# A list scheduler's view of row groups, 64-row transfers, f32 products and VectorE beside GpSimd, in a streaming encoder layer

## The chip, the cores and the metric

The kernel runs on one core of a Trainium2 chip. The metric is the device time of one execution in microseconds (us). The engines are TensorE (PE: matmuls and transposes; PEld: its weight loads), VectorE (DVE), ScalarE (ACT), GpSimd (POOL) and SyncE (SP), which here only issues DMA transfers. ScalarE issues some transfers as well. Each engine takes its own instructions strictly in the order in which the program lists them; semaphores hold an instruction back until what it needs is there.

## The reference

One layer of a streaming encoder over 2048 prompt rows and 64 sample rows of 1024 columns, all in float32:

```python
def encoder_layer(x, c, conv_hist, attend, p):
    mod = jax.nn.silu(c) @ p['w_ada'] + p['b_ada']
    sh1, sc1, gt1, sh2, sc2, gt2 = [m[:, None, :] for m in jnp.split(mod, 6, axis=-1)]
    h = rms_norm(x, p['norm1_g']) * (1 + sc1) + sh1
    z = h @ p['w_in']
    glu_a, glu_b, q, k, v, g_conv, g_attn = jnp.split(z, offs, axis=-1)
    u = glu_a * jax.nn.sigmoid(glu_b)
    conv_out, conv_state = conv_module(u, conv_hist, ...)   # depthwise conv of 31 taps, LayerNorm, swish, projection
    q = rms_norm(q.reshape(B, T, N_HEADS, HEAD_DIM), p['q_norm_g'])
    k = rms_norm(k.reshape(B, T, N_HEADS, HEAD_DIM), p['k_norm_g'])
    o = attend(q, k, v, p['rel_bias']).reshape(B, T, ATTN_DIM)   # own chunk of 64 rows and 8 before it
    merged = jax.nn.sigmoid(g_conv) * conv_out + jax.nn.sigmoid(g_attn) * (o @ p['w_attn_out'])
    x = x + gt1 * (merged @ p['w_o'])
    h2 = rms_norm(x, p['norm2_g']) * (1 + sc2) + sh2
    gate, up = jnp.split(h2 @ p['w_ffn_in'], 2, axis=-1)
    x = x + gt2 * ((jax.nn.silu(gate) * up) @ p['w_ffn_out'])
    return x, conv_state, k, v
```

`mod`, the modulation, is a product of the condition vectors c with `w_ada`. Its first two parts, `sh1` and `sc1`, are in every row of `h`, and so in everything that comes after it.

## The kernel before

**Stages.** The first stage goes through the rows in four blocks (576, 512, 512 and 512): `h` from x, the input projection, the convolution, the attention by heads, the gates. The results go to DRAM scratch. The second stage goes through them in three blocks (576, 768, 768): merge, output projection, norm, FFN. Big products are made three times with operands that are split into a high and a low part (`split`: ScalarE copies the high part, VectorE or GpSimd subtracts it), so that each weight passes through ScalarE and VectorE or GpSimd before TensorE can use it.

**The start.** `load_vectors` (line 1101) loads two small tiles: `r0` (16 rows: 8 of c_prompt, 8 of c_sample, on ScalarE's queue) and `r1` (76 rows, on SyncE's queue: norm1_g in rows 0 to 8, norm2_g to 16, b_dw to 20, conv_ln_g to 24, conv_ln_b to 28, b_ada to 76). In the trace both are called `r`. `Slabs` loads pieces of `w_ada` (`wmod`, 512 KB each, four held) on both queues in turn, `first_rows` (1227) the first 576 rows of x, on both queues, and `Weights` pieces of `w_in` (`wst`, three held). `first_block` (1232) then works in this order. TensorE transposes `r0`; ScalarE and VectorE make silu(c) of it (`cl`); TensorE multiplies `wmod` by `cl` (`mod_sums`, tile `pa`); it transposes `r1` (`vectors`), which gives `cols`; it turns the sums into columns with the 0/1 matrix `sel` (`mod_columns`), and VectorE adds `b_ada` and the gains: tiles `A` and `B`. Beside it ScalarE sums the squares of the rows of x (`junk`, `ssq`), GpSimd takes the power, VectorE scales the rows (`scale_rows`). TensorE transposes them (`turn`), VectorE applies `A` and `B` (`h`), ScalarE and VectorE split it into `hh` and `hl`, and the first product of the projection reads `hh` and `whi`.

**The planner.** The order on each engine is not that of the code. `Meter` and `Queue` hand each operation to `Plan.do` (line 239), which records it with an estimated cost; `flush` (300) puts all the operations of a stage into an order, engine by engine, with a simulation of its own, and then emits them in that order (all lines of the trace are therefore line 383). There are three flushes: line 1962, near the end of the first stage, line 1990 at its end, and line 2561 at the end of the kernel.

- `places` (177) names the regions that an operand touches. For a tile in SBUF they are groups of 32 partitions by 32 columns. Two operations that touch one region, one of them writing, get an edge. A transfer's edge is always a true wait (`deps`): it is planned only after the end of the other.
- `cost` (201) gives the time that an operation holds its engine (`occ`) and the time until its result is there (`lat`).
- `do` gives a transfer its `size`, the time that it is to take of one shared server, by its bytes and by the length of its contiguous runs.
- In `flush` each operation gets a due time, from TensorE's clock (the sum of TensorE's costs in the order of the code) backwards through all who read its result; a transfer's due time is 8 us earlier still. TensorE's operations are ranked by the order of the code, those of the other engines by due time. Then the operation that can start first is placed again and again, at equal start the one of lower rank.
- `room` (392) holds a transfer back while eight others of its queue are planned to be in flight, and an operation whose tile has no free buffer.
- `place` (407) sets start and end, and takes a transfer's size from the server.

The planner's estimates change nothing but the order. Which waits the program contains is decided by the tile framework, which tracks overlaps by itself.

Of the kernel before, what the change touches and what calls it, by code (L numbers as in the profile page):

```python
# [17 lines left out]
P = 128  # L18
# [67 lines left out]
class Meter:  # L86


    def __init__(self, engine, name, stream, plan):
        self.engine, self.name, self.stream, self.plan = engine, name, stream, plan  # L90
# [35 lines left out]

class Op:

    __slots__ = ("engine", "call", "occ", "lat", "deps", "at", "tiles", "start", "end", "need", "ready", "out", "order", "rank", "size", "clock")

    @property
    def ins(self):
# [3 lines left out]
class Rooms:  # L136
# [6 lines left out]
    def tile(self, shape, dtype, tag=None, name=None, bufs=None):  # L143
        kw = {k: v for k, v in (("tag", tag), ("name", name), ("bufs", bufs)) if v is not None}
        t = self.pool.tile(shape, dtype, **kw)
        self.plan.opened(t, (self.key, tag or name), bufs or self.bufs, self.psum)
        return t


# [9 lines left out]
class Plan:  # L159
# [3 lines left out]

    def __init__(self, tc):
        self.tc, self.on, self.ops, self.behind = tc, False, [], []
        self.clock, self.pools, self.flight = 0.0, 0, {e: [] for e in ('sp', 'act')}
        self.free = {e: 0.0 for e in ("pe", "dve", "act", "pool", "sp")}
        self.server, self.cells, self.rings, self.tiles, self.users = 0.0, {}, {}, {}, {}

    def opened(self, t, ring, bufs, psum):  # L170
        name = (t.tensor if hasattr(t, "tensor") else t).name
        r = self.rings.setdefault(ring, {"bufs": bufs, "free": [0.0] * bufs, "all": [], "due": []})
        self.tiles[name] = [ring, len(r["all"]), None, 0, psum, 0.0, False]
        r["all"].append(name)
        self.users[name] = []

    def places(self, ap):
        t = ap.tensor
        name = t.name
        info = self.tiles.get(name)  # L180
        dims = ap.ap
        if info is not None and info[4]:
            row = dims[0][0]
            a = [(ap.offset % row + st) // 512 for st in runs(dims[1:])[0]]
            n = runs(dims[1:])[1]
            return name, {(name, b) for x in a for b in range(x, x + (n + 511) // 512)}
        if info is None:
            if name.startswith(("in_", "out_")):
                return name, ()
            if name.startswith(("w_d", "sum_d", "gt_d", "rb_d")):  # L190
                return name, {(name, 0)}
            starts, run = runs(dims)
            return name, {(name, c) for a in starts for c in range((ap.offset + a) // 64, (ap.offset + a + run - 1) // 64 + 1)}
        row, count = dims[0]
        p, off = divmod(ap.offset, row)
        starts, run = runs(dims[1:])
        cells = {c for a in starts for c in range((off + a) // 32, (off + a + run - 1) // 32 + 1)}
        return name, {(name, q, c) for q in range(p // 32, (p + count - 1) // 32 + 1) for c in cells}

    @staticmethod  # L200
    def cost(engine, op, out, reads, args, kw):

        n = 1
        for d in out.shape[1:]:
            n *= d
        if op == "dma":
            return 440.0, 0.0
        if engine == "pe":
            if op == "transpose":
                occ = 108.0 if n >= 100 else 60 + 0.4 * n  # L210
            elif args[1].dtype == F32:
                occ = 54.0 if "tile_position" in kw else max(108.0, n / 0.6)
            else:
                occ = max(108.0, n / 2.4 + 13.5)
            return occ, occ + 150
        small = sum(1 for a in reads if a.shape[-1] == 1 and len(a.shape) == 2)
        if engine == "act":
            occ = 60 + 0.83 * n + 95 * (small > 0) + 190 * ("accum_out" in kw)
            return occ, occ + 120
        if engine == "pool":  # L220
            if ALU.pow in args:
                return 310 + 207 * n, 340 + 207 * n
            occ = 140 + (2.17 if op == "tensor_tensor" else 3.0) * n
            return occ, occ + 50
        if op == "reciprocal":
            return 105 + 5.5 * n, 150 + 6.1 * n
        if op == "tensor_tensor_reduce":
            occ = 135 + 1.04 * n
        elif op == "scalar_tensor_tensor":
            occ = 75 + 1.04 * n + 55 * small  # L230
        elif op in ("tensor_scalar", "tensor_copy", "memset"):
            occ = 75 + (0.5 if op != "tensor_copy" and n > 300 else 1.04) * n + 55 * small
        elif op == "tensor_reduce":
            occ = 75 + 520
        else:
            occ = 65 + 1.045 * n
        return occ, occ + 90

    def do(self, engine, op, f, args, kw):
        if not self.on:  # L240
            return f(*args, **kw)
        vals = list(args) + list(kw.values())
        out = kw.get("out", args[0] if args else None)
        writes = [out] + [kw[k] for k in ("accum_out",) if k in kw]
        reads = [a for a in vals if hasattr(a, "ap") and hasattr(a, "tensor") and not any(a is w for w in writes)]
        o = Op()
        o.engine, o.call, o.at = engine, (f, args, kw), len(self.ops)
        o.occ, o.lat = self.cost(engine, op, out, reads, args, kw)
        o.deps, o.order, o.tiles, o.out, o.start, o.rank = set(), set(), set(), [], None, float(o.at)
        o.size = 0  # L250
        self.clock += o.occ * (engine == 'pe')
        o.clock = self.clock
        if op == "dma":
            n = 4
            for d in out.shape:
                n *= d
            run = min(4 * runs(a.ap)[1] for a in (out, in_of(args)))
            o.size = n / 1024 * (47 if run >= 4096 else 50 if run >= 2048 else 53 if run >= 1024 else 58 if run >= 512 else 72) / 16
        for a in reads:
            name, cells = self.places(a)  # L260
            o.tiles.add(name)
            for c in cells:
                w = self.cells.get(c)
                if w is None:
                    w = self.cells[c] = [None, []]
                if w[0] is not None:
                    o.deps.add(w[0])
                w[1].append(o)
        for a in writes:
            name, cells = self.places(a)  # L270
            o.tiles.add(name)
            for c in cells:
                w = self.cells.get(c)
                if w is None:
                    w = self.cells[c] = [None, []]
                if w[0] is not None:
                    (o.order if w[0].engine == engine and op != "dma" else o.deps).add(w[0])
                for r in w[1]:
                    if r is not o:
                        (o.order if r.engine == engine and op != "dma" else o.deps).add(r)  # L280
                w[0], w[1] = o, []
        for b in self.behind:
            if b.engine == engine and b is not o:
                o.order.add(b)
        o.tiles = [t for t in o.tiles if t in self.tiles]
        for t in o.tiles:
            if not self.users[t]:
                insort(self.rings[self.tiles[t][0]]["due"], self.tiles[t][1])
            self.tiles[t][3] += 1
            self.users[t].append(o)  # L290
        self.ops.append(o)
        return o
# [93 lines left out]
    def end_of(self, d, o):  # L386

        if d in o.deps:
            return d.end + self.HOP + self.MARGIN.get(o.engine, 0.0) * (d.engine != o.engine)
        return d.start + d.occ  # L390

    def room(self, o, s):
# [12 lines left out]
        return s  # L405

    def place(self, o, s):
        o.start, o.end = s, s + o.lat
        self.free[o.engine] = s + o.occ
        if o.size:  # L410
            self.server = max(self.server, s + o.occ + 900) + o.size
            o.end = self.server + 1100
# [1 line left out]
        for t in o.tiles:  # L414
            info = self.tiles[t]
            r = self.rings[info[0]]
# [12 lines left out]
def in_of(args):  # L429
    return args[1]  # L430
# [506 lines left out]
def streaming_layer(ctx: ExitStack, tc: tile.TileContext, I, O):  # L937
# [289 lines left out]
    def first_rows():  # L1227
        places = ((wa, "x", 3), (wa, "x", 3), (wa, "x", 3), (wk, "kk", 1), (wk, "q2", 1))
        queues = (sync, sync, scalar, sync, scalar)
        return [load_x(*tl, *place, q) for tl, place, q in zip(token_tiles(*PBLOCKS[0]), places, queues)]  # L1230
# [1361 lines left out]
```

## Time and profile before

| | us |
|---|---|
| median of 3 runs | 2990.22 (2989.49 to 2992.82) |
| the profiled execution | 2990.09 |
| its span, from the first instruction to the last | 2988.2 |
| TensorE busy | 2903.2 |
| VectorE busy | 2060.7 |
| ScalarE busy | 1366.4 |
| GpSimd busy | 1154.2 |

The profiled execution is 1.9 us longer than its span. In the page's rows each engine's busy time stands with its share of the span. In a row of a view by stage come the window, its length, the busy time of PE, PEld, DVE, ACT and POOL with their instructions, and at the end the granted clock of TensorE, the busy share of the 16 DMA engines and their rate. In a row of waits come who waited for what, the total, the number of waits and the longest. In a chain or timeline come start, duration and what it was; "SPq" and "ACTq" are the issue of a transfer on SyncE's and ScalarE's queue. In a group row come count, busy time, mean duration in ns, then the idle time ahead of it with what ended it.

### The profile page before, as it was taken

The page shows a single profiled execution, that of the slowest core. Times are in us where ns is not written, and L with a number is a line of the kernel's source. Part 1 is how long each engine was busy: PE and PEld are TensorE (multiplying, and loading weights), DVE is VectorE, ACT ScalarE, POOL GpSimd, SP SyncE. Part 2 cuts the span into 40 slices and gives each one's busy share as a digit, 9 for nine tenths or more (in the row PEclk, how much of TensorE's full clock was granted, in tenths as well). Part 3 has the DMA queues.
Part 4 walks back from the last instruction along what each step waited for, and adds up shares of the span by engine and source line. Part 5 has one row for each costly group of instructions (what it writes and reads, how often), then busy time and mean ns, then how long its engine had stood idle before and what let it go on. Part 6 is the DMA issues. An engine that isn't in the chain of part 4 may idle for free.

```text
span 2988.2 us, 44928 instructions
## 1 busy us (share of the span) xinstructions
PE 2903.2 (97%) x16241; PEld 2591.0 (87%) x16241; DVE 2060.7 (69%) x3628; ACT 1366.4 (46%) x2459; POOL 1154.2 (39%) x752
## 2 busy tenths in 40 slices
PE   5999999999999999989999999999999999999999
PEld 3899878888888887888989899999999999999998
DVE  4898778768857885577676655676676657576666
ACT  2435643661465256464444335544444355444442
POOL 0300310111011102454556433266666842465667
PEclk8999999999999999999999999999999999999999
DMA  7899899978986977885444786433333975333333
GB/s 249 292 326 315 256 329 309 291 244 285 293 274 210 304 233 256 269 277 173 142 148 147 230 266 218 145 96 106 120 102 113 323 232 185 96 103 107 116 107 123
DMA packets 467724, 628.06 MB, mean 210 GB/s; under 512 B 36276, under 2 KB 314664, under 8 KB 467501
## 3 DMA queue, kind: packets, MB, share of 16 engines
q1 hardware_dynamic: 453456, 605.58, 62.2%
q10 hardware_dynamic: 14045, 19.60, 1.9%
q8 instruction: 128, 2.10, 0.3%
q14 instruction: 95, 0.78, 0.1%
HBM read 476.53 MB, written 148.54 MB: 209 GB/s over the span
## 4 chain that ended last, share of the span: by engine, by line
PE 88%; DMA 3%; DVE 3%; ACT 3%; issue 2%; POOL 1%; SPq 1%; DVEq 0%; POOLq 0%; ACTq 0%
PE ps L383 57%; PE pd L383 15%; PE pw L383 6%; PE po L383 2%; PE sc L383 2%; PE ptp L383 2%; DMA kk<-k_d 2%; PE pt L383 1%; PE pa L383 1%; ACT whi L383 1%; DVE wlo L383 1%; SPq L383 1%; POOL wlo L383 0%; ACT xn L383 0%; DVE pw L383 0%
## 5 line engine op out<-in xcount | busy, mean ns | idle before, releaser
L383 PE MATMUL ps<-t,whi 128*128 128x384 f32 (+1 forms) x2112 | 500.3, 322 | 5.9 <-ACT s L383 3.6
L383 POOL TENSOR_TENSOR wlo<-wst,whi 128x1024 fp32r<-128x1024 f32 (+1 forms) x160 | 365.0, 2290 | 299.2 <-ACT whi L383 256.4
L383 PE MATMUL ps<-b,whi 128*128 128x384 f32 (+1 forms) x1584 | 382.6, 327 | 12.6 <-ACT t L383 8.1
L383 ACT ACTIVATE whi<-wst 128x1024 fp32r<-128x1024 f32 (+1 forms) x264 | 256.9, 977 | 282.5 <-PE ps L383 106.5
L383 PEld LDWEIGHTS ps<-t,whi 128*128 128x128 f32 x2112 | 367.8, 188 | 13.8 <-ACT s L383 5.4
L383 DVE SCALAR_TENSOR_TENSOR y<-u,wd,y 128x512 f32<-128x512 f32 (+1 forms) x480 | 369.9, 774 | 7.9
L383 DVE TENSOR_TENSOR acc<-acc,pd 128x512 f32<-128x512 f32 (+1 forms) x482 | 324.4, 685 | 56.0 <-PE pd L383 50.1
L383 PE MATMUL ps<-hh,whi 128*128 128x512 f32 (+2 forms) x992 | 362.8, 366 | 0.0
L383 PE MATMUL ps<-hh,wlo 128*128 128x512 f32 (+2 forms) x992 | 345.2, 348 | 0.0
L383 PE MATMUL ps<-hl,whi 128*128 128x512 f32 (+2 forms) x992 | 345.1, 348 | 0.0
L383 PE MATMUL ps<-t,wlo 128*128 128x384 f32 (+1 forms) x1056 | 338.9, 321 | 0.0
L383 PE MATMUL pd<-whi,hid 128*128 128x512 f32 (+1 forms) x956 | 307.0, 390 | 0.3 <-ACT whi L383 0.3
L383 PEld LDWEIGHTS ps<-b,whi 128*128 128x128 f32 x1584 | 278.9, 190 | 19.1 <-ACT t L383 8.3
L383 POOL TENSOR_TENSOR t<-t,mhalf 128x1 f32<-128x1 f32 (+3 forms) x68 | 87.8, 1299 | 449.2 <-DVE t L383 381.0
L383 PE MATMUL ps<-b,wlo 128*128 128x384 f32 (+1 forms) x792 | 257.3, 325 | 0.0
L383 ACT ACTIVATE pr<-pr,sm 128x640 f32<-128x640 f32 (+4 forms) x272 | 200.3, 747 | 118.7 <-DVE sm L383 117.4
L383 PEld LDWEIGHTS pd<-whi,hid 128*128 128x128 f32 (+1 forms) x956 | 174.7, 183 | 41.6 <-ACT whi L383 0.8
L383 PEld LDWEIGHTS ps<-hh,wlo 128*128 128x128 f32 x992 | 186.9, 188 | 21.6
L383 PEld LDWEIGHTS ps<-hh,whi 128*128 128x128 f32 x992 | 187.5, 189 | 19.3 <-issue 2.4
L383 PEld LDWEIGHTS ps<-hl,whi 128*128 128x128 f32 x992 | 187.7, 189 | 15.9 <-issue 2.3
L383 PEld LDWEIGHTS ps<-t,wlo 128*128 128x128 f32 x1056 | 198.1, 188 | 0.1
L383 POOL TENSOR_TENSOR wlo<-ws,whi 128x512 fp32r<-128x512 f32 x96 | 122.5, 1296 | 187.1 <-ACT whi L383 187.1
(232 smaller groups left out, 6299.9 us busy)
## 6 DMA issues: line engine op xcount, KB each, us to landing
wlo<-w_din_l SPq DMA_DIRECT2D x72, 512.0 KB, 5.7
whi<-w_din_h SPq DMA_DIRECT2D x72, 512.0 KB, 6.5
wst<-sum_d SPq DMA_DIRECT2D x132, 256.0 KB, 3.0
wfo<-in_w_ffn_out SPq DMA_DIRECT2D x64, 512.0 KB, 4.2
wmod<-in_w_ada SPq DMA_DIRECT2D x46, 512.0 KB, 6.4
sum_d<-ws SPq DMA_DIRECT2D x88, 256.0 KB, 3.1
wst<-in_w_ffn_in SPq DMA_DIRECT2D x84, 256.0 KB, 3.1
wst<-in_w_in SPq DMA_DIRECT2D x40, 512.0 KB, 6.4
```

Of the source, the lines that this page charges most:

```text
L383: f(*args, **kw)
```

## The change

The change is in the class `Plan` and its helpers alone; the operations of the kernel stay as they are.

- Regions: a tile in SBUF that does not have 128 partitions is kept in groups of 4 partitions instead of 32. Such tiles are `r0`, `r1`, the raw taps and cached convolution rows, the rows of the relative bias, and the small tiles of the convolution state.
- TensorE's f32 products: 116 ns with a `tile_position` (the products of `wmod`) instead of 54; else 160 ns up to 128 columns and 455 ns above, instead of n / 0.6.
- Transfers: a transfer with 64 rows, contiguous runs of 2 KB or more and over 200,000 bytes counts 1.5 times.
- VectorE beside GpSimd: an operation that reads two large operands, neither of them in PSUM, is marked `two`. Where one on VectorE overlaps with the last six of GpSimd, it is lengthened by 0.9 of the overlap.
- A term in `end_of` that is multiplied by 0.0.

```diff
-        self.plan.opened(t, (self.key, tag or name), bufs or self.bufs, self.psum)
+        self.plan.opened(t, (self.key, tag or name), bufs or self.bufs, self.psum, 32 if shape[0] == P else 4)
...
-        return name, {(name, q, c) for q in range(p // 32, (p + count - 1) // 32 + 1) for c in cells}
+        return name, {(name, q, c) for q in range(p // info[7], (p + count - 1) // info[7] + 1) for c in cells}
...
-                occ = 54.0 if "tile_position" in kw else max(108.0, n / 0.6)
+                occ = 116.0 if "tile_position" in kw else 160.0 if n <= P else 455.0
...
+        big = [a for a in reads if a.shape[-1] >= 64 or len(a.shape) > 2]
+        o.two = len(big) > 1 and op not in ("activation",) and not any(self.tiles.get(a.tensor.name, (0,) * 5)[4] for a in big)
...
+            if out.shape[0] == 64 and run >= 2048 and n > 200000:
+                o.size *= 1.5
...
-            return d.end + self.HOP + self.MARGIN.get(o.engine, 0.0) * (d.engine != o.engine)
+            return d.end + self.HOP + 0.0 * (d.size > 0) + self.MARGIN.get(o.engine, 0.0) * (d.engine != o.engine)
...
     def place(self, o, s):
-        o.start, o.end = s, s + o.lat
-        self.free[o.engine] = s + o.occ
+        slow = 0.0
+        if o.two and o.engine == "dve":
+            slow = 0.9 * sum(max(0.0, min(b, s + o.occ) - max(a, s)) for a, b in self.shared[-6:])
+        elif o.two and o.engine == "pool":
+            self.shared.append((s, s + o.occ))
+        o.start, o.end = s, s + o.lat + slow
+        self.free[o.engine] = s + o.occ + slow
```

More of the change, by code (lines that the diff above doesn't have):

```diff
@@ L127 @@
 class Op:
-    __slots__ = ("engine", "call", "occ", "lat", "deps", "at", "tiles", "start", "end", "need", "ready", "out", "order", "rank", "size", "clock")
+    __slots__ = ("engine", "call", "occ", "lat", "deps", "at", "tiles", "start", "end", "need", "ready", "out", "order", "rank", "size", "clock", "two")
     @property
@@ L165, in __init__ @@
         self.tc, self.on, self.ops, self.behind = tc, False, [], []
+        self.shared = []
         self.clock, self.pools, self.flight = 0.0, 0, {e: [] for e in ('sp', 'act')}
@@ L168, in __init__, with opened @@
         self.server, self.cells, self.rings, self.tiles, self.users = 0.0, {}, {}, {}, {}
-    def opened(self, t, ring, bufs, psum):
+    def opened(self, t, ring, bufs, psum, step):
         name = (t.tensor if hasattr(t, "tensor") else t).name
         r = self.rings.setdefault(ring, {"bufs": bufs, "free": [0.0] * bufs, "all": [], "due": []})
-        self.tiles[name] = [ring, len(r["all"]), None, 0, psum, 0.0, False]
+        self.tiles[name] = [ring, len(r["all"]), None, 0, psum, 0.0, False, step]
         r["all"].append(name)
```

## The prediction

> **What bounds the kernel now.** I read the page first, then one view of busy time by stage, then TensorE's waits, then the first 46 us as a chain and instruction by instruction. The change touches only the planner, so what counts is where TensorE stands still: an order can remove idle time, not work.
>
> ```profile
> span 2988.2 us, 44928 instructions
> PE 2903.2 (97%) x16241; PEld 2591.0 (87%) x16241; DVE 2060.7 (69%) x3628; ACT 1366.4 (46%) x2459; POOL 1154.2 (39%) x752
> ```
>
> The stages (busy us of PE, PEld, DVE, ACT, POOL after each window's length, then clock, DMA share, GB/s):
>
> ```profile
> 0.00:44.00 44.00, 8.36 (x48) 4.14 (x48) 14.28 (x44) 13.25 (x28) 4.22 (x12) 0.79 0.80 261
> 44.00:100.00 56.00, 56.00 (x358) 41.39 (x359) 33.54 (x72) 15.56 (x25) 11.73 (x8) 0.95 0.77 265
> 100.00:1250.00 1150.00, 1125.36 (x6396) 961.99 (x6395) 868.21 (x1647) 561.92 (x1058) 169.36 (x140) 0.99 0.86 281
> 1250.00:2988.00 1738.00, 1713.50 (x9443) 1583.48 (x9441) 1144.69 (x1867) 775.63 (x1348) 968.88 (x592) 1.00 0.49 161
> ```
>
> TensorE idles 2988.2 - 2903.2 = 85.0 us. Of that 44 - 8.36 = 35.6 lie in the first 44 us, none in the next 56, 24.6 in the rest of stage one, 24.5 in the 1738 us after it. Who is waited for:
>
> ```profile
> PE pt L383 <- DMA r<-in_c_sample: 17.1, 1, 17.1
> PE pt L383 <- DMA wst<-in_w_in: 11.1, 1, 11.1
> PE ps L383 <- ACT t L383: 9.1, 2, 8.1
> PE sc L383 <- DMA kk<-k_d: 7.0, 6, 3.2
> ```
>
> The two longest waits stand ahead of transposes of `r0` (the c vectors) and `r1` (norm gains and biases): TensorE waits for loads of 2 to 24 KB. The second is put down to a weight load, but the instruction reads `r1`, so I take the last row of `r1`, b_ada. Here is the chain of the start, and then TensorE, ScalarE's queue and SyncE's queue in order of time:
>
> ```profile
> 1.66 8.21 DMA wmod<-in_w_ada
> 9.89 7.03 DMA r<-in_c_sample
> ...
> 38.29 0.16 DVE A L383
> ```
>
> ```profile
> 17.06 0.26 PE L383 MATMUL pt<-ident,r 16*128 16x16 f32 x1 [17.06 <-DMA r<-in_c_sample]
> 18.25 3.64 PE L383 MATMUL pa<-wmod,cl 128*32 128x256 f32 x32 [0.93 <-DVE cl L383]
> 34.50 0.36 PE L383 MATMUL pt<-ident,r 76*128 76x76 f32 x1 [11.09 <-DMA wst<-in_w_in]
> 43.96 1.54 PE L383 MATMUL ps<-whi,hh 128*64 128x512 f32 x3 [1.04 <-ACT hh L383]
> ```
>
> ```profile
> 9.89 0.29 ACTq L383 DMA_DIRECT2D r<-in_c_sample  x1
> 13.49 0.30 SPq L383 DMA_DIRECT2D r<-in_norm_g  x1
> 16.54 0.28 SPq L383 DMA_DIRECT2D r<-in_b_dw  x1
> 22.37 0.40 SPq L383 DMA_DIRECT2D r<-in_conv_ln_g  x1
> 28.58 0.47 SPq L383 DMA_DIRECT2D r<-in_conv_ln_b  x1
> 29.71 0.45 SPq L383 DMA_DIRECT2D r<-in_b_ada  x1
> ```
>
> The pieces of one 76-row tile leave SyncE one by one over 29 us (the first norm_g at 0.7). That is the planner's order: rows are kept in groups of 32, so norm1_g (rows 0-8), norm2_g, b_dw, ln_g and ln_b (to row 28) and b_ada (28-76) seem to overwrite each other, and each is planned only after the one before has landed. c_sample stands behind c_prompt likewise. The chip pays because SyncE issues in that order, each issue behind whatever the queue waits for.
>
> A second thing sets these times. c_sample is the 13th transfer issued, and it left at 9.89, when the fifth one landed (1.66 + 8.21 = 9.87). So I read that an issue also waits for the landing of the transfer eight before it, over both queues together.
>
> **The change part by part.**
>
> *Groups of 4 rows (the one large term).* All eight pieces begin at multiples of 4, so every false wait between them goes. `rank` then sorts them by due time, TensorE's use less the steps between and less the transfer: wmod feeds TensorE's first products, x goes through five steps (squares, sum, power, scaling) before it is transposed, the vectors through few, and the first wst is used last. I expect on ScalarE's queue c_prompt, c_sample, two wmod, two x_t; on SyncE's two wmod, three x_t, the six vectors, and only then the first wst. What is late next?
>
> ```profile
> DMA packets 4667, 7.05 MB, mean 294 GB/s; under 512 B 263, under 2 KB 3323, under 8 KB 4667
> x_t<-in_x_prompt ACTq DMA_DIRECT2D x2, 512.0 KB, 12.7
> x_t<-in_x_prompt SPq DMA_DIRECT2D x2, 512.0 KB, 10.8
> 17.68 0.61 ACT L383 ACTIVATE junk<-x_t 64x512 f32<-64x512 f32 x1
> 24.26 0.61 ACT L383 ACTIVATE junk<-x_t 128x512 f32<-128x512 f32 x1
> ```
>
> The first row is the traffic of the first 24 us. (1) wmod (2 MB) and x (2.25 MB) still come first: 4.25 MB at 294 GB/s is 14.5 us. c_sample no longer matters, so the products with wmod start when wmod is in, at some 12 to 14 us in place of 18.25. (2) The last vector is some 18th in order, so it waits for the 10th, an x_t issued near 2.5 to 5 and landing 10.8 to 12.7 later: issue at 14 to 16, and 2 to 3 us more to land (only other vectors are queued ahead of it): 17 to 18. Then transpose and copy; `r1` is turned at about 18 in place of 34.50: 16.5 us. (3) From that transpose to the first product is 43.96 - 34.50 = 9.5 us (A and B, the scaling of x, five transposes, h, hh). It stays: 27.5. (4) The ten squares on ScalarE take 24.87 - 17.68 = 7.2 us; from 13.5 they end by 21 to 22 as the last x lands near 16; the first weight's split follows, about 1 + 1.2 us: 24.5. That is before 27.5, so hidden. The first product goes from 43.96 to about 27: -17.
>
> Of this something comes back. The next three sets of wmod and the wst loads, spread over a half-idle DMA before, are now needed 17 us sooner. By 44 us before 44 x 261 = 11.5 MB had moved; at 294 to 350 GB/s 27 us carry 7.9 to 9.5. What TensorE truly needs by its second set of products is 7.75 MB (eight wmod, x, three wst), so it is close; I give back 3 us. Sum for the start: **-14**. Ends: nothing (the vectors land late all the same), and -22 (first product at 16 + 5.7, when all that remains is the first 4.75 MB and the tail from A at 38.29 to 43.96).
>
> *64-row transfers counted 1.5 times.*
>
> ```profile
> q<-q_d SPq DMA_DIRECT2D x64, 256.0 KB, 5.1
> kk<-k_d SPq DMA_DIRECT2D x48, 256.0 KB, 6.0
> vv<-v_d SPq DMA_DIRECT2D x24, 512.0 KB, 6.6
> ```
>
> 64 + 48 loads are planned some 0.4 us longer (256 KB x 50/16 = 0.8 us). The trace supports it: 256 KB in 64 rows takes nearly as long as 512 KB in 128. No instruction is added. What it can win is the 7.0 us that scores wait for `kk`; what it can lose is a score planned later than it could run. Ends -7 and +7; I take -1.
>
> *Costs of the f32 products.*
>
> ```profile
> 53.48 0.44 PE pa L383 x4
> 58.95 1.43 PE pa L383 x24
> ```
>
> One product leaves two records. The 12 of wmod take 1.43/12 = 119 ns; the new 116 fits where 54 did not. The two with `sel` take 220 ns, and the new 160 fits worse than the old 213. There are 192 of the first kind and 32 of the second: in the plan's clock 192 x 62 = 11.9 us more, 32 x 53 = 1.7 less. They lie before 780 us, where TensorE is full: nothing, ends -2 and +2.
>
> *VectorE beside GpSimd.*
>
> ```profile
> L383 DVE TENSOR_TENSOR sums<-s,sums 128x384 fp32r<-128x384 f32 x18 | 21.8, 1213 | 26.9 <-ACT sums L383 26.9
> L383 DVE TENSOR_TENSOR sums<-ps,sums 128x384 fp32r<-128x384 f32 x54 | 29.6, 548 | 0.0
> L383 DVE SCALAR_TENSOR_TENSOR y<-u,wd,y 128x512 f32<-128x512 f32 x360 | 268.6, 750 | 6.1
> L383 DVE SCALAR_TENSOR_TENSOR part_l<-pt,gqk,part_h 128x512 fp32r<-128x512 f32 x32 | 23.8, 745 | 6.3 <-DMA k_d<-part_l 2.8 <-ACT part_h L383 2.5 <-DMA c_d<-part_l 0.7
> ```
>
> The effect is real: with both inputs in SBUF the first takes 1213 ns, with one in PSUM 548. It matters after 1250, where GpSimd is busy 969 of 1738 us, and there TensorE is full but for 24.5 us, of which one wait for `t` is 8.1 (the chain of norm and transposes on entering the FFN). In stage one the taps take 750 beside 745, no slowing to speak of. Ends -6 and +6; I take nothing. The `0.0 *` term in `end_of` is nothing.
>
> Sum: -14 - 1 = -15 from the profiled execution's 2990.1 (0.1 below the median of 2990.2): **2975**.
>
> **The rivals.**
>
> *The vectors land late anyway.* Against my 18 us speaks that 4 KB of c_sample took 7.03 us with large loads ahead of it on its queue. If the six are ranked behind three x_t and the first wst and each is seven us under way, b_ada lands at about 23, the first product at 33: -11, with 3 given back -8: 2982. The Trainium skill (DMA: Bandwidth & Descriptors, section Queues, rings and completion order) has a rule for it: each DMA engine takes descriptors of a ring in order. By that rule a 2 KB load behind 2.5 MB is as late as the 2.5 MB, and the trace agrees for c_sample (7.03).
>
> *Given back before 1250.* Stage one's DMA share is 0.86 on average. If it were the bound, weights would come no sooner and TensorE would idle later: about 2988. Against: 1150 x 0.86 = 989 us of transfer leave 161 us, and the waits for DMA there are few (7.0).
>
> *Slower.* Scores are planned later for the longer q and `kk` loads, so the one `kk` buffer is freed later, its next load is issued later, and the wait feeds itself in each of the 24 heads of blocks 1 to 3. At 1 us per head that is +24 and -15: 2999. It decides from (15 + 6)/24 = 0.9 us per head on. Against: now all waits for `kk` together are 7.0 us in 6 places, and TensorE has other products to fill with.
>
> *It doesn't do what it says.* If the planner's room in flight, not the groups, sets the vectors' order, nothing moves: 2990. Against: eight transfers fit in flight, and c_prompt to c_sample needs only two.
>
> **How the numbers follow.** Forecast 0.62 (own range 2966 to 2982), vectors late 0.15 (two thirds of it beyond -6), given back 0.10, slower 0.08, nothing 0.05. About 0.2%, 6 us, is what a measurement can tell from no change. Faster: 0.62 + 0.10 = 0.72; same: 0.05 + 0.10 + 0.05 = 0.20; slower 0.08. The small terms' ends (-7 and -6 beside -22 for the start) seldom fall together; with the start's best and one of them the time is near 2962. Upwards the range takes in the late vectors and given-back cases: 2962 to 2989.
>
> **What would show it.** Right: c_sample among the first four transfers on ScalarE's queue, b_ada issued before 17 us, the first wmod product before 15, the 76-row transpose near 18, the first product of `hh` near 27, and idle of TensorE from 44 to 1250 still about 25 us. Wrong: b_ada after 22; or an early first product followed by new waits for `wmod` or `wst` before 100 us; or waits for `kk` above 15 us in total. The prediction fails above all if the new order of stage one, which I can't see, idles TensorE over 10 us more or less than the 24.6 now.

## The result, and the profile after

| | before | after |
|---|---|---|
| median of 4 runs | 2989.85 us (2987.42 to 2992.82) | 2955.41 us (2953.45 to 2960.99) |
| the profiled execution | 2990.09 | 2954.55 |
| ratio, 95% interval | | 0.9887 (0.987 to 0.9905) |

The changed kernel is 34 us faster. The forecast was 15 us faster; the range, from 2962 us, missed the time by 7 us at its lower end. The page after, and its view by stage (columns as in the rows of before):

```profile
span 2952.7 us, 44886 instructions
PE 2897.3 (98%) x16241; PEld 2590.4 (88%) x16241; DVE 2056.5 (70%) x3628; ACT 1361.9 (46%) x2459; POOL 1152.6 (39%) x752
```

```profile
0.00:44.00 44.00, 24.94 (x154) 14.96 (x158) 20.71 (x61) 14.34 (x31) 4.22 (x12) 1.00 0.85 265
44.00:100.00 56.00, 55.63 (x344) 42.82 (x337) 38.01 (x71) 19.61 (x31) 13.94 (x11) 1.00 0.96 327
100.00:1250.00 1150.00, 1134.95 (x6516) 976.53 (x6515) 872.38 (x1671) 572.85 (x1084) 187.00 (x148) 1.00 0.87 284
1250.00:2952.00 1702.00, 1681.76 (x9235) 1556.13 (x9234) 1125.38 (x1827) 755.10 (x1315) 947.49 (x581) 1.00 0.49 159
```

The reader subtracts busy from length and compares. TensorE's idle time fell from 85.0 to 55.4 us: by 16.2 in the first 100 us, by 9.6 from there to 1250 (24.64 to 15.05), by 4 behind that. And its busy time fell, from 2903.2 to 2897.3, with the same 16241 products. In these two executions idle alone does not make the difference; 5.9 us of it are products that ran faster. How much of the 5.9 the change brings, one trace of each does not show: e3 below, no faster than before by its median, has 2898.5 us of busy time in its own trace.

The start came at the times that were forecast. TensorE's first steps after, then SyncE's issues and one of ScalarE's, in order of time:

```profile
4.77 0.26 PE L388 MATMUL pt<-ident,r 16*128 16x16 f32 x1 [4.77 <-DMA r<-in_c_sample]
13.40 3.64 PE L388 MATMUL pa<-wmod,cl 128*32 128x256 f32 x32 [8.38 <-DVE cl L388]
...
18.88 0.33 PE L388 MATMUL pt<-ident,r 76*128 76x76 f32 x1
...
27.66 1.54 PE L388 MATMUL ps<-whi,hh 128*64 128x512 f32 x3 [1.04 <-ACT hh L388]
```

```profile
6.10 0.34 SPq L388 DMA_DIRECT2D r<-in_b_ada  x1
9.71 4.29 SPq L388 DMA_DIRECT2D r<-in_norm_g  x2
14.05 0.30 SPq L388 DMA_DIRECT2D r<-in_b_dw  x1
15.03 0.25 SPq L388 DMA_DIRECT2D r<-in_conv_ln_g  x1
15.32 0.29 SPq L388 DMA_DIRECT2D r<-in_conv_ln_b  x1
```

```profile
11.09 0.30 ACTq L388 DMA_DIRECT2D rv<-in_rel_bias  x1
```

All six vectors leave between 6 and 16 us, the 76-row tile is turned at 18.88 in place of 34.50, and the first product comes at 27.66 in place of 43.96. From 44 to 100 us TensorE idles 0.4 us. Two of the times came another way than forecast, which is luck. The products with `wmod` start at 13.40, as forecast, but their row waits for `cl`, not for `wmod`: ScalarE, which makes `cl`, stood at the issue of `rv` (the relative bias) until 11.09. And the 76-row transpose at 18.88 has no wait in its row: it waits for no vector, but stands behind the products with `wmod` and `sel` in TensorE's order.

Most of what the prediction did not have lies in stage one. TensorE's largest waits there (who waited for whom, us in total, number, longest; "issue" is idle time for which the profile shows no cause), first the rows of before for scores (`sc`) beside the 7.0 us for `kk`, then after:

```profile
PE sc L383 <- DVE sm L383: 5.5, 3, 4.9
PE sc L383 <- issue: 4.4, 3, 1.9
```

```profile
PE sc L388 <- DVE sm L388: 8.1, 4, 3.2
PE ptp L388 <- ACT pr L388: 2.7, 2, 1.8
PE sc L388 <- issue: 1.6, 2, 1.1
```

The 7.0 us of scores waiting for `kk` are gone altogether. What scores wait for VectorE (`sm`) grew by 2.6 us, what they wait without a cause shown fell by 2.8.

**A wait can cost more than its length.** Here are TensorE's instructions of before around one of those waits, and the view of that stretch (before, after its length the busy times, then clock, DMA share, GB/s):

```profile
1145.98 0.48 PE L383 MATMUL ps<-hh,whi 128*128 128x512 f32 x1
1149.62 1.40 PE L383 MATMUL sc<-kk,q 128*128 128x320 f32 x4 [3.16 <-DMA kk<-k_d]
1150.82 0.63 PE L383 MATMUL ps<-hl,whi 128*128 128x512 f32 x1
1151.24 0.63 PE L383 MATMUL ps<-hh,wlo 128*128 128x512 f32 x1
...
1155.79 0.40 PE L383 MATMUL ps<-hl,whi 128*128 128x512 f32 x1
1156.02 0.40 PE L383 MATMUL ps<-hh,wlo 128*128 128x512 f32 x1
```

```profile
1149.50:1156.00 6.50, 6.38 (x21) 5.45 (x22) 2.93 (x6) 1.60 (x4) 0.00 (x0) 0.53 1.06 379
```

From 1149.6 to about 1155.6 a product follows the one before it after 0.42 us; afterwards it is 0.23. The granted clock is 0.53. Six microseconds at half speed are some 3 us of work lost on top of the 3.16 of idle, and they are booked as busy time. The Trainium skill (TensorE: Matmul & The Clock Gate, section What's actually happening) says that the array's clock falls to half after about one idle window of 3.4 us and needs about a busy one to come back. The trace agrees in kind: half clock after 3.16 us of idle, for some 6 us. Not every wait of that length has this behind it. In e14 (below) scores wait 3.30 us for `kk` at 1149.78, and from there a product follows the one before it after 0.23 us, at a granted clock of 1.00.

### The profile page after: what moved, and what is told of

The parts are those of the page before. It is cut to its first block, busy times and chain, and to the rows that moved or that the text cites. A ratio compares the mean times of both kernels' runs of the same rounds, so it can differ in the third digit from the quotient of the medians.

```text
span 2952.7 us, 44886 instructions
## 1 busy us (share of the span) xinstructions
PE 2897.3 (98%) x16241; PEld 2590.4 (88%) x16241; DVE 2056.5 (70%) x3628; ACT 1361.9 (46%) x2459; POOL 1152.6 (39%) x752
## 4 chain that ended last, share of the span: by engine, by line
PE 89%; DVE 4%; ACT 2%; DMA 2%; issue 1%; POOL 1%; SPq 0%; ACTq 0%; DVEq 0%; POOLq 0%
PE ps L388 59%; PE pd L388 16%; PE pw L388 6%; PE po L388 2%; PE sc L388 2%; PE ptp L388 2%; PE pt L388 1%; PE pa L388 1%; ACT whi L388 1%; DVE wlo L388 1%; DMA wst<-in_w_in 1%; DVE y L388 0%; POOL wlo L388 0%; DVE pw L388 0%; POOL ws L388 0%
## 5 line engine op out<-in xcount | busy, mean ns | idle before, releaser
L388 DVE TENSOR_TENSOR acc<-acc,pd 128x512 f32<-128x512 f32 (+1 forms) x482 | 324.4, 685 | 55.4 <-PE pd L388 49.7
```

## The experiments

Each of the edits below is made alone or left out alone. To read where an experiment's time went, I cut each profiled run at these marks: the first product of `hh`, the first product of the merge (tile `pw`), the first of the down projection (`pd`), the last `pw` product with weights, and the end of the span. The lengths between them, in us (stage one is the length from the first product of `hh` to the merge):

| profiled run | first product at | stage one | merge to `pd` | to last `pw` | to the end | median of its runs |
|---|---|---|---|---|---|---|
| before | 44.0 | 1178.8 | 138.7 | 1130.3 | 496.4 | 2989.85 |
| groups (e1) | 25.6 | 1182.3 | 139.6 | 1130.3 | 496.4 | 2974.55 |
| 64-row transfers (e5) | 43.8 | 1163.9 | 139.6 | 1129.9 | 496.4 | 2975.41 |
| VectorE beside GpSimd (e17) | 44.3 | 1174.6 | 135.9 | 1128.2 | 495.3 | 2979.21 |
| three costs, no groups (e2) | 43.0 | 1162.4 | 136.3 | 1128.0 | 495.2 | 2965.92 |
| after without transfers (e6) | 28.0 | 1178.1 | 136.9 | 1127.8 | 495.2 | 2966.37 |
| after without VectorE (e7) | 28.4 | 1165.5 | 139.7 | 1130.1 | 496.4 | 2963.66 |
| after without f32 costs (e8) | 25.4 | 1167.2 | 136.7 | 1128.1 | 495.5 | 2954.24 |
| after | 27.7 | 1165.1 | 137.0 | 1127.7 | 495.2 | 2955.41 |

Each of three edits has columns of its own. The groups move the first product. The transfers shorten stage one. VectorE beside GpSimd shortens the three stretches behind it: from the merge to `pd` the eight traces with that edit have 135.2 to 137.0 us, the twelve without it 138.2 to 140.1. Each row is one trace, and stage one is the less steady length: in the trace of e3, where nothing that matters was changed, it is 1173.3, 5.5 below before's.

**Is it the start, the costs, or chance?** e1 has the groups alone, e2 the three costs alone, e4 the groups and the transfers; e3 changes one number that means nothing here.

```diff
-    HOP, MARGIN = 60.0, {"pe": 150.0}
+    HOP, MARGIN = 64.0, {"pe": 150.0}      # e3; e11: the same on after
```

> Before, with the groups of 4 rows alone; the planner's costs are those of before. Theory S (all 35 us come from the start: 16 us of idle at the start, 6 us of TensorE time that a cold clock cost, and an order of everything behind it that is planned from the right point): about 2957. Theory C (the start gives only its 16 us, the other 18 us come from the three costs): about 2973. Theory N (the rest is chance: any new order moves the time by some 10 us either way): 2973, off by up to 10.

> Before, with the three costs (f32 products, 64-row transfers, VectorE beside GpSimd) and with groups of 32 rows as before. Theory S: 2990, no change, with the first product of hh still near 44 us. Theory C: about 2972. Theory N: 2990, off by up to 10.

> Before, with one number of the planner's that means nothing here changed: 64 ns instead of 60 between an operation and its reader. It measures how far an order that is merely different moves the time. Theories S and C: within 3 us of before, 2987 to 2993. Theory N: 5 to 15 us off, either way, with the start unchanged.

> Groups of 4 rows, and 64-row transfers counted 1.5 times; the other two costs as before. Theory S: as the groups alone. Theory C: 5 to 8 us below the groups alone, and fewer waits of scores for kk than before's 7.0 us. Theory N: up to 10 us off the groups alone, either way.

Measured, beside 2991.73 for before: e1 2974.55, ratio 0.994 (0.9927 to 0.9954); e2 2965.92, 0.9911 (0.9898 to 0.9925); e3 2990.31, 0.9993 (0.9984 to 1.0002); e4 2963.6, 0.9906 (0.9892 to 0.9919). Theory S falls: the costs alone bring 26 us with the first product still at 43 us. Theory N falls as well, for these sizes: one merely different order moved the time by 1.4 us. Theory C stands, and gave 2972 for e2 where 2966 came: the costs alone are worth more than the 18 us that were left to explain. The edits do not add up: the groups are worth 17 us alone, but 10.5 on top of the costs (2965.92 to 2955.41). e4 is 11 us below e1, more than the 5 to 8 expected, and none of its scores wait for `kk`.

**Which cost?** e5 has the transfers alone; e6, e7 and e8 are after without the transfers, without VectorE's slowing, without the f32 products; e17 has VectorE's slowing alone.

```diff
+            if out.shape[0] == 64 and run >= 2048 and n > 200000:    # only this in e5, left out in e6
+                o.size *= 1.5
...
+            slow = 0.9 * sum(...)       # only this part in e17, left out in e7
...
-                occ = 116.0 if "tile_position" in kw else 160.0 if n <= P else 455.0    # e8: back to the old costs
+                occ = 54.0 if "tile_position" in kw else max(108.0, n / 0.6)
```

> Before, with 64-row transfers counted 1.5 times as the only edit. On top of the groups this edit gave 11 us (2974.6 to 2963.6), where the prediction had 1. If that is what the edit itself is worth, it gives it here too: 2990 - 11 = 2979, with the waits of scores for kk (7.0 us in six places before) gone and the first product of hh still near 44 us. If it only pays with the early start: 2990.

> After, without the 1.5 of the 64-row transfers (they count as before). If the transfers are the second large term: about 2955 + 9 = 2964 or more, with waits of scores for kk back at 5 us or more in total. If the other two costs carry the gain as well as it does: 2955 to 2958.

> After, without VectorE's slowing beside GpSimd. The prediction has nothing for it: 2955 to 2957. The costs alone gave 26 us and the transfers 11 of them, so some 14 are to be shared by this edit and the next: if it is this one, about 2963 to 2969.

> After, with the f32 products at their old costs (54 ns, and n / 0.6). The prediction has nothing for it: 2955 to 2957. If the planner's clock of TensorE is what brings the 14 us that neither the start nor the transfers explain: 2963 to 2969. The start comes up to 2 us sooner than in after, as in the groups alone (first product at 25.6 us).

> Before, with VectorE's slowing beside GpSimd alone. If the 8 us that after loses without it are its own: 2982 to 2985, with stage one as before (first pw product at 1220 to 1225) and some 6 us less from there to the end. If they come only together with the other edits: 2990.

e5: 2975.41, ratio 0.9945 (0.9933 to 0.9958). e6: 2966.37, 0.9916 (0.9903 to 0.993). e7: 2963.66, 0.9911 (0.9896 to 0.9926). e8: 2954.24, 0.9875 (0.9862 to 0.9889). e17: 2979.21, 0.9959 (0.9946 to 0.9971). In these runs before had 2990.6 to 2991.9.

So the transfers are worth 16.5 us alone and 11 in after, and VectorE's slowing 11.4 alone and 8.3 in after. (After was timed beside another set of runs of before; by the ratios the two are worth 8.7 and 7.2 in after.) The f32 products are worth nothing: without them after is, if anything, 1 us faster, and its first product comes 2.3 us sooner. In e6 the scores wait for `kk` again:

```profile
PE sc L386 <- DMA kk<-k_d: 8.5, 7, 3.8
```

In e17 some 6 of the 11 us lie behind stage one, as expected, and some 4 in stage one, which I had not expected. Those 4 are not in the waits: TensorE's idle time in stage one is 25.0 us, in before 24.6, and its busy time there fell by 4.6 us, as it did in e3's trace (by 5.1) without a gain. Where they come from stays open. Behind stage one idle time fell by 4 us, from 24.7 to 20.8. The longest wait is the one on entering the FFN. First two rows of e7, without the edit, then three of e17:

```profile
PE ps L385 <- ACT t L385: 8.1, 1, 8.1
PE ps L385 <- DVE v L385: 3.3, 3, 2.6
```

```profile
PE ps L386 <- ACT t L386: 5.4, 1, 5.4
PE ps L386 <- DVE t L386: 2.2, 1, 2.2
PE ps L386 <- DVE v L386: 1.6, 1, 1.6
```

With this edit that wait is 5.4 us in both after and e17; without it, 8.1 in before, e1 and e7. But with the edit a second one of 2.2 us, for VectorE's `t`, stands right behind it; in e7 that is 0.2. So the entry to the FFN gives some 0.7 us, and the rest of the 4 is spread over smaller waits (`v` from 3.3 to 1.6). Which instructions on VectorE changed places to bring this I did not find out.

**Why do the transfers gain so much?** Two theories: the scores are now planned when q and `kk` are really there (P), or the server, which all transfers share in the plan, is fuller, and all others move (Q). e9 lets a 64-row transfer land later in the plan by half its size and leaves the server; e10 holds the server longer and lets the transfer itself land as before.

```diff
+            o.more = 0.5 * o.size if out.shape[0] == 64 and run >= 2048 and n > 200000 else 0.0
...
             self.server = max(self.server, s + o.occ + 900) + o.size
-            o.end = self.server + 1100
+            o.end = self.server + 1100 + o.more                            # e9; in e13 o.more is 1600.0
+            self.server += o.more           # e10: this line, behind the old o.end
```

> Before, with the 64-row transfers planned to land later by half their size, while the server (and so every transfer behind them) keeps its old times. Theory P (the gain of 16 us comes from scores that are planned when q and kk are really there, so that TensorE is given other products ahead of them): 2975 to 2979, with the waits of scores for kk gone. Theory Q (it comes from a fuller server, which moves all transfers): 2990.

> The other half: the server is held 1.5 times as long by a 64-row transfer, but that transfer itself is planned to land as before; only those behind it land later. Theory P: little of the 16 us, 2985 to 2990, waits of scores for kk at 4 us or more (some is left, as a kk load behind another is later). Theory Q: 2975.

e9 came to 2986.22, ratio 0.9992 (0.9983 to 1.0), e10 to 2976.57, 0.996 (0.9947 to 0.9973), beside 2989.47. Read as written, that is Q. But the two don't part the theories. A head's four loads (q and `kk`, twice) go out one behind the other, so in e10 the last of them is planned 3 x 0.4 = 1.2 us later too, and in e9 only 0.4. And in e10 the waits for `kk` are gone, as P says; its profiled run was the slowest of its five, with one wait of 4.4 us for a weight. So e13 moves these loads alone, by as much as the full edit moves the last of the four, and e14 all the others and not these.

```diff
+            self.plain = max(self.plain, s + o.occ + 900) + o.size         # e14
+            self.server = max(self.server, s + o.occ + 900) + o.size + o.more
+            o.end = (self.plain if o.more else self.server) + 1100
```

> Before, with every long 64-row transfer planned to land 1.6 us later (four times the 0.4 us by which the last of a head's four loads moves in the full edit), the server as before. Theory P (scores planned when q and kk are really there): 2974 to 2980, no waits of scores for kk. Theory Q (the fuller server moves the other transfers): 2985 to 2990, as e9.

> Before, with the server held 1.5 times as long by these transfers for all others, while they themselves are planned to land as before. Theory P: 2986 to 2992, with waits of scores for kk at 4 us or more. Theory Q: 2974 to 2980.

e13: 2975.67, ratio 0.9947 (0.9935 to 0.996). e14: 2991.11, 1.0003 (0.9994 to 1.0012). Before had 2990.59. Theory P it is: planning only the long 64-row transfers 1.6 us later brings 15 of the edit's 16.5 us, and a fuller server for the others brings nothing. The waits of scores in stage one, first e13, then e14:

```profile
PE sc L384 <- DVE sm L384: 6.0, 4, 3.7
PE sc L384 <- DMA kk<-k_d: 2.7, 1, 2.7
```

```profile
PE sc L385 <- DMA kk<-k_d: 11.8, 7, 3.3
PE sc L385 <- DVE sm L385: 5.3, 4, 2.6
PE sc L385 <- issue: 3.1, 2, 2.3
```

One wait for `kk` is left in e13, though I had expected none.

**More of the same?** e18 is after without the f32 costs (e8), with 2.0 in place of 1.5.

> After without the f32 products' costs (2954.2), and 64-row transfers counted 2.0 times instead of 1.5. If scores still wait for loads that are planned too short: 2948 to 2952. If 1.5 has them all covered (no wait for kk is left in after): 2952 to 2958, no gain.

2961.41, ratio 0.9902 (0.9887 to 0.9917): worse than e8's 0.9875, and than what I gave it. Stage one takes 1175.5 us in place of 1167.2, with no wait for `kk` at all; instead the scores wait for VectorE, and the transposes of the softmax for ScalarE (in e8 4.2 and 2.9 us):

```profile
PE sc L388 <- DVE sm L388: 9.2, 7, 4.2
PE ptp L388 <- ACT pr L388: 4.7, 6, 1.4
```

I read this as scores planned too late, with all that hangs on them late as well; it is one run. Of the three factors tried, 1.5 is the best, and the longest is not.

**Which tile makes the start?** e15 has the small groups for `r0` alone, e16 for `r1` alone (the call is shortened; the first line is that of the full change).

```diff
-        self.plan.opened(..., 32 if shape[0] == P else 4)
+        self.plan.opened(..., 4 if shape[0] == 16 else 32)      # e15; e16: 76
```

> Groups of 4 rows for r0 (the c vectors) alone. By the prediction's chain the first product hangs on r1 (turned at 34.5 us): TensorE's first transpose comes at some 8 us in place of 17, the wmod products at some 12, and then it waits for r1 as before: 2987 to 2992. If c_sample had set the start: 2980 or less.

> Groups of 4 rows for r1 (norms and biases) alone. c_sample comes late as before (TensorE's first transpose at 16 to 17 us, the wmod products at 18 to 22), so r1 is turned at some 22 us by TensorE's order and the first product comes at about 31: 2990 - 13 = 2977, range 2974 to 2980. If r1 is not what the start hangs on: 2988 or more.

e15: 2996.84, ratio 1.0014 (1.0004 to 1.0024), beside 2990.59. As expected `r0` alone wins nothing; it is even 6 us slower by the median, beyond the range given (2987 to 2992): b_ada leaves later, at 34.69, and the first product comes at 48.84. e16: 2988.12, 0.9992 (0.9983 to 1.0001), where 2977 was expected. Its first product does come early, at 29.75, but hardly anything is left of that at the end. Where it went, first e16, then e1 with both tiles, by stretches of 20 us:

```profile
40.00:60.00 20.00, 19.49 (x115) 12.98 (x114) 12.68 (x26) 4.79 (x6) 0.00 (x0) 1.00 1.02 321
60.00:80.00 20.00, 16.58 (x91) 10.52 (x90) 8.16 (x19) 2.43 (x3) 0.50 (x3) 0.83 0.98 354
```

```profile
40.00:60.00 20.00, 20.00 (x137) 12.05 (x134) 10.24 (x19) 5.23 (x6) 0.00 (x0) 1.00 0.97 298
60.00:80.00 20.00, 19.22 (x120) 16.11 (x117) 15.83 (x35) 9.71 (x17) 10.21 (x8) 1.00 0.91 344
```

In e16 TensorE idles 3.4 us from 60 to 80, at a clock of 0.83, while the DMA engines are busy all the time. But what it waits for there is VectorE, and no row from 40 to 90 us names a transfer:

```profile
PE pa L383 <- DVE R L383: 2.5, 1, 2.5
```

Stage one as a whole takes 1193.5 us, 14.7 more than before's: about 7 of idle time (31.5 beside 24.6) and 7 of busy time. It looks like the give-back that the prediction feared, but that the full DMA is its cause isn't shown; an order that fits worse further on would do as well. The 17 us of the groups need both tiles.

**Chance, and a better version.** e11 repeats e3's number on after. e12 is e8 with the load of the relative bias put behind the first tanh, as in after this load holds ScalarE until 11.09 and TensorE waits 8.4 us for `cl`.

```diff
-        scalar.dma_start(rv, I["rel_bias"].rearrange("l h r -> (l h) r"))
+        with behind(th_done[0]):
+            scalar.dma_start(rv, I["rel_bias"].rearrange("l h r -> (l h) r"))
```

> After, with 64 ns for 60 between an operation and its reader: how far an order that is merely different moves the time of after. The same change moved before by -1.4 us (2990.3 beside 2991.7). If the single edits' worth (17, 11 to 16 and 8 us) is their own and no chance: 2952 to 2959. If 8 us can come from a new order alone: 5 us or more away from 2955.

> After without the f32 products' costs (2954.2 in its own run), and with the load of the relative bias (rv) put behind the first tanh on ScalarE's queue, where it now waits for a landing and keeps ScalarE from the tanh. If that wait is on the path: the wmod products start up to 3 us sooner and the time is 2951 to 2953. If the last vector (r1) sets the first product anyway: 2954, the first product again at 25.4 us.

e11: 2955.79, ratio 0.9888 (0.9875 to 0.9902). e12: 2954.39, 0.988 (0.9865 to 0.9895). The same as after, and the same as e8, with the first product at 25.3 us. But e12 hardly tested the wait: in e8, from which it starts, `rv` leaves at 8.84 and not at 11.09, the products with `wmod` start at 11.20, and without `rv` ahead of them at 10.85. What the wait costs in after is not shown. No version here beats after by more than a measurement can tell.

## Why the prediction was wrong

Right, step by step, was the large term. The prediction had c_sample among the first four on ScalarE's queue (second), b_ada out before 17 us (6.1; the last vector at 15.3), the first wmod product before 15 (13.40), the 76-row transpose near 18 (18.88) and the first product near 27 (27.66). Not every reason for these times was right: the products with `wmod` were held by `cl` and not by `wmod`, and the transpose by TensorE's order. The sum for the start was -14 (-17, with 3 given back); e1, with the groups alone, measures -17. Nothing shows of the 3 us within 100 us; e1's stage one is 3.5 us longer than before's, which is less than the 5.5 between before and e3.

Two terms were mis-sized, and they are nearly the whole error of 19 us. Put in one after the other (e1, e4, e8, after), the groups bring 17 us, the transfers 11, VectorE's slowing 9, and the f32 products cost 1; the sum had 14, 1, 0 and 0.

- The 64-row transfers: "I take -1", with ends of -7 and +7. They are worth 11 us in after and 16.5 alone. The prediction named the mechanism and its 7.0 us of waits, and then took a seventh of them. It should have taken them all, since the rows showed that these loads land later than planned. Even so it would have been short. In e5's trace TensorE's idle time goes from 85.0 to 2973.6 - 2897.8 = 75.8, by 9.2, of which 8.1 in stage one; its busy time goes from 2903.2 to 2897.8, by 5.4. Whether the half clock behind the waits is this second part is argued from the one wait above and not shown: e3's trace has nearly as little busy time (2898.5) without the edit.
- VectorE beside GpSimd: "I take nothing", ends -6 and +6. It is worth 8.3 in after, some 6 of them behind stage one, where the prediction held TensorE for full but for 24.5 us. It was full, but 4 of those 24.5 us could go, over several waits: the one of 8.1 us that it named fell to 5.4 and 2.2. The rest is busy time, and its cause is open.

The step that failed is the same in both cases: the sum counted the planner's errors as if they cancelled ("Ends -6 and +6; I take nothing"), though both edits moved an estimate towards what the trace shows. The range had the same fault. It held that the small terms' best ends "seldom fall together"; both were passed, with 11 beyond 7 and 8.3 beyond 6, while the start stayed near its forecast. And the first premise, that "an order can remove idle time, not work", left no place for busy time, which the same products spend more or less of.

The f32 products at nothing were right (e8: 1 us, within the intervals), the fit of 160 for `sel` being worse than before's included. The rival of late vectors did not come: b_ada left at 6.10, right behind the x loads, and the last vector at 15.32. Slower scores, the rival on the other side, did not come at 1.5, and e18 shows its beginning at 2.0. The rival of giving back did not come here; e16's longer stage one is like it, with its cause open.

## What to carry to other kernels

Where an order is planned from estimates, the estimates that run short for a resource in the way of the busiest engine are the ones to correct first; a change that brings such an estimate nearer to the trace's number is worth the waits it ends, and it is no coin toss. Price a wait of TensorE by its length, and look at the spacing of the products behind it for what it may cost on top. And a planner that sees regions coarser than the program's writes will put waits of its own into the order, which no row of waits names as such: look for small transfers that leave one by one.

## What the runs showed of the hardware

- In before, a wait of 3.16 us was followed by some 6 us of products at half rate (clock 0.53); in e14, one of 3.30 us by products at full rate (clock 1.00). So a wait of this length may or may not cost the clock.
- The clock in the rows can miss a half rate: after, it stands at 1.00 over the first 44 us, but the first three products of `hh` take 1.54 us there, as in before at 0.50.
- TensorE's busy time for the same 16241 products lies between 2894.2 us (e2) and 2910.6 us (e16) in the twenty traces, and it does not follow the medians.
- An issue on SyncE's or ScalarE's queue stood until an earlier transfer had landed, and held ScalarE's own work as long: after, `rv` left at 11.09, when the piece of `wmod` issued at 1.70 had landed (1.70 + 9.37 = 11.07). That it is the transfer eight before, over both queues, fits c_sample in before (9.89 and 9.87).
- Single runs of one kernel scatter by some 0.5%: 27 runs of before lay between 2984.04 and 2998.83, and e3's eleven between 2983.84 and 2993.18. The medians of before lay between 2989.47 and 2991.93.
